# Conv transposes and dt steps placed behind chosen projection products, and dt results stored by direction, in a Fourier and SSD mixer layer

## The chip, the cores and the metric

One core of a Trainium2 chip runs the whole layer in one launch. The metric is the device time in microseconds. TensorE is called PE, VectorE DVE, ScalarE ACT, GpSimd POOL and SyncE SP; all transfers here are issued by SP, in its program order.

## What is computed

One layer over 2048 latent and 256 context tokens of width 1024. The normed and modulated input is multiplied by one input projection, whose columns are split five ways; two mixers read them, and one output projection adds the result to the input.

```python
u, zf, zs, xbc, dt_raw = jnp.split(h @ w_in, PROJ_SPLITS, axis=-1)
four = fourier_mixer(u, zf, w_fourier, b_fourier)
xbc = depthwise_conv_grid(xbc, conv_w, conv_b, rows, cols)
ssd, h_f, h_b = ssd_mixer(xbc, dt_raw, zs, dt_bias, a_log, d_skip, ssd_norm_w, h0_f, h0_b)
```

`dt` is softplus(dt_raw + bias) for 24 heads and two directions. The SSD scan works on chunks of 128 tokens: 16 of the latent sequence and 2 of the context. It needs, for each chunk, the cumulative sum of dt x A, its total, and exponentials of them. The convolution is a depthwise 3 x 3 over a 32 x 64 grid (over one row of 256 for the context), with a SiLU.

## The kernel before

A product of two float32 operands is made of three TensorE products of high and low parts (hh x wh, hl x wh, hh x wl), so a projection of one channel tile (128 channels) over 512 tokens is 24 products of 128x512 (L170 to L172). The program is written with a tile framework: buffers come from pools with a fixed count, and a scheduler decides, within the dependencies, in which order each engine's instructions stand. An engine's order is then fixed, and an instruction that waits holds up all that stand behind it on that engine. `tc.issue_after(x)` adds edges: what is created under it stands behind instruction x.

The stages that the change touches, with their times in the profile:

- The u stage, about 116 to 275 us. A loop over n2 in 0..15 (L465) projects 128 tokens on 512 channels with 24 u-products (L474 to L476), splits the result, and multiplies it by a DFT matrix with three products (L482 to L484) into a "tr" accumulator, which DVE copies to "gs" (L486) for a store. The context block (`ctx_block`, called at n2 = 2) transposes the normed context (L236), splits it on DVE, ACT and POOL (L238, L72, L68), and makes its dt_raw (L252, L253). `dt_part(i)` is called at n2 = 4, 7 and 10, each for six of the 18 chunks. It loads transposed dt_raw from DRAM into "ev" buffers, of which there are two (L412), adds bias and softplus on DVE and ACT after products with an identity (L414), makes cumulative sums and totals on PE (L433, L436), stores four results to `sm_d` (L447), and transposes the cumulative sum and the log of dt less that sum by groups of up to four chunks (L455); ACT and DVE write the high and low halves of each group to "ev" (L457, L458), which are stored to `cum_d` and `q_d`.
- The conv stage, about 270 to 835 us. `conv_tile` is called for 20 channel tiles in CONV_ORDER (a C, a B and three x tiles, four times). A tile has four blocks of 512 tokens; ACT copies each block to an image (`img`), of which there are two. `finish(half)`, called after block 2 and block 3, lets ACT make the first tap (L561), DVE the other eight (L564), and ACT the SiLU (L567), on one of two "acc" buffers (four "cacc" and "acc" in all, by kind). It returns a function that transposes the eight token tiles (L509), copies them (L511) and stores them; B tiles also multiply with the C tile's result (L539) and reduce its diagonal on POOL and DVE (L544, L545) to `cbd`. These functions wait in a list, `late`, and one is called after each odd block. x and B tiles end with the context: 24 products, two taps, SiLU (L604), two transposes.
- The start of the scan, about 820 to 905 us. `zf_tile(2)` projects one more tile; then `sml`, `ecb` and `dtb2` are loaded from `sm_d`, DVE makes `dsc` from `dtb2` and `cbd` (L631), and the scan steps begin, with projections of zs tiles between them and gate steps (L757 to L764) that load a weight each.

PSUM has five "mm" accumulators for projections (`main_psum`), two "tr" ones (`tr_psum`) and one for the context. The later stages are the rest of the scan (to about 1160 us), the Fourier mixer (to about 1300) and the output stage; of the change they see only where the dt results are loaded from, and a slightly different order.

Of the kernel before, what the change touches and what calls it, by code (L numbers as in the profile page):

```python
# [18 lines left out]
P = 128  # L19
# [7 lines left out]
H = 24  # L27
# [22 lines left out]
def mixer_layer(ctx: ExitStack, tc: tile.TileContext, A: dict, out: bass.AP, taps=None):  # L50
# [36 lines left out]
    sm_d = scratch("sm_d", [NALL, P, 4, W2])  # L87
# [68 lines left out]

    def weights(idx, raw=None):
# [9 lines left out]
    def project_k(po, w, hi, lo, c0, n, k):  # L167
        wh, wl = w
        a, b = hi[:, k, c0:c0 + n], lo[:, k, c0:c0 + n]
        mm(po, wh[:, k], a, start=(k == 0), stop=False)  # L170
        mm(po, wh[:, k], b, start=False, stop=False)  # L171
        mm(po, wl[:, k], a, start=False, stop=(k == KT - 1))  # L172
# [177 lines left out]
    with ExitStack() as pu:  # L350
# [48 lines left out]
        def dt_part(i):  # L399
            sl = slice(NH * i, NH * i + NH)  # L400
# [3 lines left out]

            def bc(t):
                return t.unsqueeze(1).broadcast_to([P, NH, W2])

            pt = tr_psum([P, NH, W2])
            for q0 in range(0, NH, 4):
# [3 lines left out]
                for q in range(nq):  # L413
                    mm(pt[:, q0 + q, :], dtT[:, q * P:(q + 1) * P], D0["i2"], start=True, stop=True)  # L414
            v, e, u, s1_, dtt, wdec, etot, ecum = (D0[t].rearrange("p (c w) -> p c w", w=W2) for t in
                                                   ("v", "e", "u", "s1", "dtt", "wdec", "etot", "ecum"))
            nc.vector.tensor_tensor(out=v, in0=pt, in1=bc(D0["dtb"]), op=ALU.add)
# [11 lines left out]
            da, cum = u, e  # L429
            nc.vector.tensor_tensor(out=da, in0=dtt, in1=bc(D0["nega"]), op=ALU.mult)  # L430
            pt = tr_psum([P, NH, W2])
            for d, tri in enumerate(("triu", "tril")):
                mm(pt[:, :, d * H:(d + 1) * H], D0[tri], da[:, :, d * H:(d + 1) * H], start=True, stop=True)  # L433
            nc.vector.tensor_copy(out=cum, in_=pt)
            pt = tr_psum([P, NH, W2])
            mm(pt, D0["ones"], da, start=True, stop=True)  # L436
            nc.scalar.activation(etot, pt, AF.Exp)
            nc.vector.tensor_tensor(out=wdec, in0=pt, in1=cum, op=ALU.subtract)
            nc.scalar.activation(wdec, wdec, AF.Exp)
            nc.vector.tensor_tensor(out=wdec, in0=wdec, in1=dtt, op=ALU.mult)  # L440
            nc.scalar.activation(ecum, cum, AF.Exp)
            lq = v
            nc.vector.tensor_scalar(out=lq, in0=dtt, scalar1=1e-37, scalar2=None, op0=ALU.max)
            nc.scalar.activation(lq, lq, AF.Ln)
            nc.vector.tensor_tensor(out=lq, in0=lq, in1=cum, op=ALU.subtract)
            for q, t in enumerate((wdec, etot, ecum, dtt)):
                store(sm_d[sl, :, q].rearrange("c p w -> p c w"), t)  # L447
            for src, dst in ((cum, cum_d), (lq, q_d)):
                c0 = NH * i
                while c0 < min(NH * (i + 1), NCH):  # L450
                    nq = min(4, min(NH * (i + 1), NCH) - c0)
                    n = nq * P
                    pt = tr_psum([W2, 512])
                    for q in range(nq):
                        nc.tensor.transpose(pt[:, q * P:(q + 1) * P], src[:, c0 + q - NH * i], ident)  # L455
# [7 lines left out]

        dt_consts()
        for n2 in range(16):  # L465
            if n2 == 2:
                ctx_block()
            if n2 in (4, 7, 10):
                dt_part((n2 - 4) // 3)
            po = main_psum()  # L470
            for k in range(KT):
# [4 lines left out]
                mm(po, b, wuh[:, k], start=False, stop=(k == KT - 1))  # L476
# [14 lines left out]
    with ExitStack() as pc_:  # L491
# [57 lines left out]
        def conv_tile(n, ci):  # L549
# [34 lines left out]
            for b in range(4):  # L584
# [20 lines left out]
            (x_tokens if kind == "x" else b_tokens)(acc, j, NCH, NCC)  # L605

        late = []
# [12 lines left out]
    sml = pers.tile([P, NALL, 2, W2], F32, name="sml")  # L620
    ecb = pers.tile([P, NCH, H], F32, name="ecb")
    dsc = pers.tile([P, NCH, G, HG], F32, name="dsc")

    zf_tile(2)
    dtb2 = pers.tile([P, NCH, H], F32, name="dtb2")
    dsk = const_tile("dskip", pers)
    smr = sm_d[:].rearrange("c p i w -> p c i w")
    load(sml, smr[:, :, 0:2])
    load(ecb, smr[:, :NCH, 2, H:])
    load(dtb2, smr[:, :NCH, 3, H:])  # L630
    nc.vector.tensor_tensor(out=dsc, in0=dtb2[:].rearrange("p c (g h) -> p c g h", g=G),  # L631
# [695 lines left out]
```

## Time and profile before

| | |
|---|---|
| median of three runs | 1951.25 us (1950.36 to 1951.3) |
| profiled execution | 1953.2 us, of which the span is 1951.2 us |
| mean granted PE clock | 0.979 |
| DVE, ACT, POOL busy | 70%, 44%, 47% of the span |
| DMA | 269.77 MB in 279,826 packets, 138 GB/s |

In lines of the profile a group is named by the source line, the engine, the operation and output <- inputs. In a line of waits, "PE ptr L482 <- DVE ev L458" says that PE's instruction of line 482 stood still until DVE's of line 458 was done. The time of a wait is idle time of the waiting engine only.

### The profile page before, as it was taken

The numbers are of one execution on the slowest core, as the hardware profiler recorded it, in microseconds if no ns is written. First come the engines' busy times: TensorE is split into PE (matmuls) and PEld (weight loads), VectorE is DVE, ScalarE is ACT, GpSimd is POOL, SyncE is SP. The second block draws the span as 40 slices with busy tenths as digits, with TensorE's granted clock in tenths as the row PEclk, the third lists the DMA queues.
The fourth block names the chain that finished last, engine by engine and source line by source line (L and its number), as shares of the span: only waits on it lengthen the run. The fifth ranks groups of instructions, "written<-read, shape, count | busy, mean of one in ns | idle before, by whom it ended". The sixth has DMA issues, their size and how long they took to land.

```text
span 1951.2 us, 27816 instructions
## 1 busy us (share of the span) xinstructions
PE 1826.5 (94%) x9142; PEld 1498.0 (77%) x9142; DVE 1374.8 (70%) x1830; ACT 863.6 (44%) x1940; POOL 919.3 (47%) x766
## 2 busy tenths in 40 slices
PE   6999799999999998998999999988899999999997
PEld 2798687787887887877788886865678777777776
DVE  3743357999898998947666641357878887778874
ACT  3631124443444444425566654335544444444442
POOL 1321023314114023137777762256877776777742
PEclk9999799999999999998999999999999999999998
DMA  7332322323223233276777766476544444444441
GB/s 275 138 102 57 77 77 78 104 76 106 73 68 102 71 90 106 63 210 188 224 221 237 215 196 218 146 226 202 163 131 147 137 140 131 138 143 134 139 141 40
DMA packets 279826, 269.77 MB, mean 138 GB/s; under 512 B 38818, under 2 KB 247586, under 8 KB 279171
## 3 DMA queue, kind: packets, MB, share of 16 engines
q1 hardware_dynamic: 279682, 268.00, 45.7%
q8 instruction: 73, 1.20, 0.3%
q14 instruction: 71, 0.57, 0.1%
HBM read 181.37 MB, written 86.54 MB: 137 GB/s over the span
## 4 chain that ended last, share of the span: by engine, by line
PE 33%; DVE 24%; POOL 8%; DMA 7%; issue 6%; ACT 4%; SPq 1%; POOLq 0%; ACTq 0%; DVEq 0%
DVE acc L564 17%; PE po L1167 5%; PE po L1165 5%; PE po L1166 5%; PE pj L171 3%; PE pj L172 3%; PE pj L170 3%; PE py L1106 2%; DMA wo<-in_wout 2%; DMA xt<-xtok_d 2%; POOL yb L730 1%; PE parg L1032 1%; POOL xw L710 1%; SPq L63 1%; POOL wl L72 1%
## 5 line engine op out<-in xcount | busy, mean ns | idle before, releaser
L564 DVE SCALAR_TENSOR_TENSOR acc<-img,c_convw,acc 128x1024 f32<-128x1024 f32 x320 | 478.8, 1511 | 32.9 <-ACT acc L561 24.3
L172 PE MATMUL pj<-hh,wl 128*128 128x512 f32 x1152 | 456.6, 396 | 0.9 <-POOL wl L72 0.9
L171 PE MATMUL pj<-hl,wh 128*128 128x512 f32 x1152 | 455.5, 395 | 0.0
L170 PE MATMUL pj<-hh,wh 128*128 128x512 f32 x1152 | 452.3, 396 | 0.0
L72 POOL TENSOR_TENSOR wl<-raw,wh 128x1024 fp32r<-128x1024 f32 x48 | 123.7, 2578 | 443.1 <-ACT wh L68 443.1
L172 PEld LDWEIGHTS pj<-hh,wl 128*128 128x128 f32 x1152 | 218.2, 189 | 47.5 <-POOL wl L72 1.5
L170 PEld LDWEIGHTS pj<-hh,wh 128*128 128x128 f32 x1152 | 218.9, 190 | 41.1 <-issue 1.2
L171 PEld LDWEIGHTS pj<-hl,wh 128*128 128x128 f32 x1152 | 218.5, 190 | 41.3 <-issue 1.6
L1165 PE MATMUL po<-hl,mh 128*128 128x512 f32 x384 | 155.6, 405 | 4.6 <-ACT mh L68 2.1
L1166 PE MATMUL po<-hh,mh 128*128 128x512 f32 x384 | 152.5, 397 | 2.2 <-DVE hh L810 2.2
L1167 PE MATMUL po<-hl,ml 128*128 128x512 f32 x384 | 146.0, 398 | 1.5 <-POOL ml L72 1.5
L727 ACT ACTIVATE xd<-xt,dsc 128x64 f32<-128x64 f32 x384 | 101.1, 336 | 82.8 <-POOL yb L730 80.7
L1032 PE MATMUL parg<-rt,lt 128*128 128x384 f32 x256 | 90.0, 374 | 14.8 <-DVE parg L1034 10.5
L1036 ACT ACTIVATE w<-parg 128x384 f32<-128x384 f32 x128 | 62.3, 487 | 89.8 <-DVE parg L1034 89.4
L567 ACT ACTIVATE acc<-acc,c_convb 128x1024 f32<-128x1024 f32 x40 | 46.1, 1152 | 116.8 <-DVE acc L564 116.8
L72 POOL TENSOR_TENSOR ml<-gt,mh 128x384 fp32r<-128x384 f32 x64 | 68.8, 1075 | 60.6 <-ACT mh L68 58.2
L710 POOL TENSOR_TENSOR xw<-xt,sml 128x384 f32<-128x384 f32 x76 | 67.0, 883 | 53.8 <-DVE xl L72 38.9
L1037 DVE TENSOR_TENSOR w<-w,cb 128x768 f32<-128x768 f32 x64 | 83.3, 1301 | 12.2 <-ACT w L1036 11.4
L68 ACT ACTIVATE xh<-xw 128x384 fp32r<-128x384 f32 x136 | 70.0, 515 | 47.9 <-POOL xw L710 18.4
L1075 POOL TENSOR_TENSOR ts<-ts,yb 128x384 f32<-128x384 f32 x64 | 71.4, 1116 | 40.9 <-issue 16.3
L1034 DVE COPY_PREDICATED parg<-msk,parg 128x384 f32<-128x384 uint8 x128 | 70.8, 553 | 26.5 <-PE parg L1032 26.3
L72 POOL TENSOR_TENSOR sl<-hf,sh 128x384 fp32r<-128x384 f32 x64 | 77.4, 1210 | 22.8 <-ACT sh L68 19.9
(375 smaller groups left out, 4044.2 us busy)
## 6 DMA issues: line engine op xcount, KB each, us to landing
raw<-in_win SPq DMA_DIRECT2D x48, 512.0 KB
xt<-xtok_d SPq DMA_DIRECT2D x80, 192.0 KB
xtok_d<-tk SPq DMA_DIRECT2D x48, 256.0 KB
zsT_d<-ev SPq DMA_DIRECT2D x48, 256.0 KB
yb_d<-yb SPq DMA_DIRECT2D x64, 192.0 KB
yb<-yb_d SPq DMA_DIRECT2D x64, 192.0 KB
zs<-zsT_d SPq DMA_DIRECT2D x64, 192.0 KB
xg<-xtok_d SPq DMA_DIRECT2D x64, 192.0 KB
```

The lines of the kernel that those rows point to most:

```text
L72: (lo_engine or nc.vector).tensor_tensor(out=lo, in0=src, in1=hi.bitcast(F32), op=ALU.subtract)
L170: mm(po, wh[:, k], a, start=(k == 0), stop=False)
L171: mm(po, wh[:, k], b, start=False, stop=False)
L172: mm(po, wl[:, k], a, start=False, stop=(k == KT - 1))
L564: nc.vector.scalar_tensor_tensor(out=acc, in0=im[:, r0 + dy:r0 + dy + 16, dx:dx + GRID_W], scalar=tap(t), in1=acc, op0=ALU.mult, op1=ALU.add)
L710: nc.gpsimd.tensor_tensor(out=xw, in0=xt, in1=wd, op=ALU.mult)
L727: nc.scalar.activation(xd[:, h], d["x"][:, h], AF.Copy, scale=dsc[:, c, g, h:h + 1])
L1032: mm(po, l[:, dr], r[:, cols], start=True, stop=True)
L1037: nc.vector.tensor_tensor(out=w, in0=w, in1=cb[:].unsqueeze(1).broadcast_to([P, HG, P]), op=ALU.mult)
L1165: mm(po, a, wh[:, i], start=(g == 0 and q == 0), stop=False)
L1166: mm(po, a, wl[:, i], start=False, stop=False)
L1167: mm(po, b, wh[:, i], start=False, stop=(g == 3 and q == 3))
```

## The change

Three things are done.

First, `dt_part` is cut into three steps: `dt_soft` (load, identity products, softplus), `dt_cum` (sums, exponentials, stores) and `dt_rows` (transposes, splits, stores). For part i they are called at n2 = 3 + 4i, 5 + 4i and 6 + 4i, each behind an edge from the last u-product of that n2. Their accumulators come from the five "mm" buffers instead of the two "tr" ones.

Second, in the conv stage the transposing functions go into two lists by block. `flush` calls them behind an edge from the last projection product before it: after block 1 those of the first half, after block 3 those of the second half and of the context, each of the tile before. The last z_f tile is moved into the conv section, so that the last conv tile's functions stand behind its blocks 1 and 3.

Third, `sm_d` becomes `smf_d` and `smb_d`, one for each direction, with the partition first. A dt part writes seven stores instead of four; the scan loads `smb` (one run of 6912 bytes for each partition) and the two context chunks of `smf` instead of `sml`, `ecb` and `dtb2`, and `dsc` is made in place in a part of `smb`. The output stage loads 288 bytes for each partition and chunk instead of 768.

The core of the diff:

```diff
-            pt = tr_psum([P, NH, W2])
+            pt = dt_psum()
...
             for q, t in enumerate((wdec, etot, ecum, dtt)):
-                store(sm_d[sl, :, q].rearrange("c p w -> p c w"), t)
-            for src, dst in ((cum, cum_d), (lq, q_d)):
+                if q < 3:
+                    store(smf_d[:, sl, q], dview(t)[:, 0])
+                store(smb_d[:, q, sl], dview(t)[:, 1])
+
+        def dt_rows(i):
+            for src, dst in ((D0["e"], cum_d), (D0["s1"], q_d)):
...
+                    pt = main_psum()[:W2]
...
+        dt_work = {3 + 4 * i + q: (fn, i) for i in range(3) for q, fn in ((0, dt_soft), (2, dt_cum), (3, dt_rows))}
         for n2 in range(16):
             if n2 == 2:
                 ctx_block()
-            if n2 in (4, 7, 10):
-                dt_part((n2 - 4) // 3)
...
+                mu = mm(po, b, wuh[:, k], start=False, stop=(k == KT - 1)).ins
+            if n2 in dt_work:
+                fn, i = dt_work[n2]
+                with tc.issue_after(mu):
+                    fn(i)
...
-                if b % 2 and late:
-                    late.pop(0)()
+                if b % 2:
+                    flush(b)
                 if b == 2:
-                    late.append(finish(0))
+                    late[1].append(finish(0))
                 if b == 3:
-                    late.append(finish(1))
+                    late[3].append(finish(1))
...
-            (x_tokens if kind == "x" else b_tokens)(acc, j, NCH, NCC)
+            late[3].append(lambda: (x_tokens if kind == "x" else b_tokens)(acc, j, NCH, NCC))
...
+        def flush(b):
+            with tc.issue_after(done["mm"]):
+                while late[b]:
+                    late[b].pop(0)()
+
         for n, ci in enumerate(CONV_ORDER):
             conv_tile(n, ci)
-        for fn in late:
-            fn()
+        w = weights(6)
+        for b in range(4):
+            plain_block(w, b, AF.Silu, zf_sink(2))
+            if b % 2:
+                flush(b)
...
-    load(sml, smr[:, :, 0:2])
-    load(ecb, smr[:, :NCH, 2, H:])
-    load(dtb2, smr[:, :NCH, 3, H:])
+    load(smf, smf_d[:, NCH:, 0:2])
+    load(smb, smb_d)
```

How the order moves. In the u stage, around part 0 of before (line 433 makes the cumulative sums, 455 the row transposes, 482 to 484 the DFT products), PE's rows are:

```order
L433 MATMUL ptr<-wh,wl 128x6x24 x2
L436 MATMUL ptr<-wh,wl 128x288
L455 MATMUL ptr<-c_ident,wh 48x128 x12
L482 MATMUL ptr<-uh,h_dft_1088 128x512
L483 MATMUL ptr<-ul,h_dft_1088 128x512
L484 MATMUL ptr<-uh,l_dft_1089 128x512
```

and around the row transposes of the second part after (line 472; 490 to 492 are u-products, 502 to 504 the DFT):

```order
L491 MATMUL pj<-wul,hh 128x512
L492 MATMUL pj<-wuh,hl 128x512
L472 MATMUL pj<-c_ident,wh 48x128 x6
L472 MATMUL pj<-c_ident,wl 48x128 x6
L502 MATMUL ptr<-uh,h_dft_1089 128x512
L503 MATMUL ptr<-ul,h_dft_1089 128x512
L504 MATMUL ptr<-uh,l_dft_1090 128x512
L490 MATMUL pj<-wuh,hh 128x512
```

The sums (now line 446) have left the row transposes by 24 products, and u-products of the next n2 follow one DFT triple behind the transposes.

The context block stood among u-products in before (236 transposes, 252 and 253 dt products):

```order
L474 MATMUL pj<-wuh,hh 128x512
L236 MATMUL ptr<-c_ident,rawu 128x128
L236 MATMUL ptr<-c_ident,rawv 128x128
L475 MATMUL pj<-wul,hh 128x512
L252 MATMUL pc<-hch,wdt 96x256
L476 MATMUL pj<-wuh,hl 128x512
L474 MATMUL pj<-wuh,hh 128x512
L236 MATMUL ptr<-c_ident,rawu 128x128
L236 MATMUL ptr<-c_ident,rawv 128x128
L253 MATMUL pc<-hcl,wdt 96x256
```

Now its transposes (239) and dt products (255, 256) follow each other with no u-product between them; the first softplus product stands behind them:

```order
L239 MATMUL ptr<-c_ident,rawu 128x128
L239 MATMUL ptr<-c_ident,rawv 128x128
L239 MATMUL ptr<-c_ident,rawu 128x128
L239 MATMUL ptr<-c_ident,rawv 128x128
L255 MATMUL pc<-hch,wdt 96x256
L239 MATMUL ptr<-c_ident,rawu 128x128
L239 MATMUL ptr<-c_ident,rawv 128x128
L256 MATMUL pc<-hcl,wdt 96x256
L255 MATMUL pc<-hch,wdt 96x256
L239 MATMUL ptr<-c_ident,rawu 128x128
```

In the conv stage, at the boundary of two x tiles, ACT's rows in before (561 is the first tap, 567 the SiLU of a half; "tk" copies are those of transposed tokens, "img" those of projected blocks):

```order
L68 ACTIVATE img_2030<-pj 128x8x64
L68 ACTIVATE tk<-ptr 128x512 x2
L561 ACTIVATE acc<-img_2030,c_convw 128x1024
L68 ACTIVATE img_2030<-pj 128x8x64
L68 ACTIVATE tk<-ptr 128x256
L68 ACTIVATE img_2030<-pj 128x8x64
L567 ACTIVATE acc<-acc,c_convb 128x1024
```

and after, at such a boundary (581 is the first tap, 587 the SiLU):

```order
L68 ACTIVATE img_2040<-pj 128x8x64
L68 ACTIVATE tk<-ptr 128x512 x2
L581 ACTIVATE acc<-img_2040,c_convw 128x1024
L587 ACTIVATE acc<-acc,c_convb 128x1024
L68 ACTIVATE img_2040<-pj 128x8x64 x2
L68 ACTIVATE tk<-ptr 128x512 x2
L581 ACTIVATE acc<-img_2040,c_convw 128x1024
```

The two token copies of a half stand behind the image copy of block 1 and then behind that of block 3, and the first tap of a half follows them at once. On PE this is a set of eight transposes after every 48 projections; in before the sets of the repeating part stood 34 to 38 projections after the one before within a tile, and some 47 after it from tile to tile, among the context products.

At the end of the stage the last tile's two halves now stand between the blocks of the last z_f tile and the last context transposes 24 products later, and the first scan steps stand with 47 projections among them (64 before), after which nine follow without a projection between (seven before).

More of the change, by code (lines that the diff above doesn't have):

```diff
@@ L155, in ctx_psum @@
         return ps.tile([P, CTX], F32, name="pc", tag="cx", bufs=1)
+    done = {}
     def weights(idx, raw=None):
@@ L171, in project_k @@
         mm(po, wh[:, k], b, start=False, stop=False)
-        mm(po, wl[:, k], a, start=False, stop=(k == KT - 1))
+        done["mm"] = mm(po, wl[:, k], a, start=False, stop=(k == KT - 1)).ins
     def project(po, w, hi, lo, c0, n):
@@ L413, in dt_part @@
                 for q in range(nq):
[L414 to L417, printed above, removed]
+                    mm(dview(pt)[:, :, q0 + q], dtT[:, q * P:(q + 1) * P], D0["i2"], start=True, stop=True)
+            v, e, u, s1_, dtt = (D0[t] for t in ("v", "e", "u", "s1", "dtt"))
+            nc.vector.tensor_tensor(out=dview(v), in0=dview(pt), in1=dbc("dtb"), op=ALU.add)
             nc.vector.scalar_tensor_tensor(out=e, in0=v, scalar=-1.0, in1=v, op0=ALU.mult, op1=ALU.max)
@@ L428, in dt_part, with dt_cum @@
             nc.vector.scalar_tensor_tensor(out=dtt, in0=v, scalar=0.0, in1=s1_, op0=ALU.max, op1=ALU.add)
-            da, cum = u, e
-            nc.vector.tensor_tensor(out=da, in0=dtt, in1=bc(D0["nega"]), op=ALU.mult)
-            pt = tr_psum([P, NH, W2])
+            nc.vector.tensor_tensor(out=dview(u), in0=dview(dtt), in1=dbc("nega"), op=ALU.mult)
+        def dt_cum(i):
+            da, cum, lq = (D0[t] for t in ("u", "e", "v"))
+            dtt, wdec, etot, ecum = (D0[t] for t in ("dtt", "wdec", "etot", "ecum"))
+            pt = dt_psum()
@@ L619, in mixer_layer, with scan_sm @@
     pers = pool("pers", stack=pp_)
[L620 to L625, printed above, removed]
-    dsk = const_tile("dskip", pers)
-    smr = sm_d[:].rearrange("c p i w -> p c i w")
-    load(sml, smr[:, :, 0:2])
-    load(ecb, smr[:, :NCH, 2, H:])
-    load(dtb2, smr[:, :NCH, 3, H:])
-    nc.vector.tensor_tensor(out=dsc, in0=dtb2[:].rearrange("p c (g h) -> p c g h", g=G),
-                            in1=cbd[:].unsqueeze(3).broadcast_to([P, NCH, G, HG]), op=ALU.mult)
-    dv = dsc[:].rearrange("p c g h -> p c (g h)")
+    smb = pers.tile([P, 4, NALL, H], F32, name="smb")
+    smf = pers.tile([P, NCC, 2, H], F32, name="smf")
+    dsk = const_tile("dskip", pers)
+    load(smf, smf_d[:, NCH:, 0:2])
+    load(smb, smb_d)
+    dv = smb[:, 3, :NCH]
+    dv4 = dv.rearrange("p c (g h) -> p c g h", g=G)
+    nc.vector.tensor_tensor(out=dv4, in0=dv4, in1=cbd[:].unsqueeze(3).broadcast_to([P, NCH, G, HG]), op=ALU.mult)
     nc.vector.tensor_tensor(out=dv, in0=dv, in1=dsk[:].unsqueeze(1).broadcast_to([P, NCH, H]), op=ALU.add)
+    def scan_sm(dr, q, c, g):
+        t = smb[:, q, c] if dr else smf[:, c - NCH, q]
+        return t[:, g * HG:(g + 1) * HG].unsqueeze(2).broadcast_to([P, HG, 64])
     zw = {}
@@ L1007, in s1 @@
         if g == 0:
-            sml = wa1.tile([P, 4, W2], F32, name="sml4", tag="sml")
-            load(sml, sm_d[c])
+            sml = wa1.tile([P, 3, H], F32, name="sml4", tag="sml")
+            load(sml, smf_d[:, c])
         else:
```

52 lines of the change are left out of this document (27 added, 25 removed).

## The prediction

> **What bounds the kernel now.** I read the page's engine table first, then windows stage by stage, then the waits of TensorE (PE), and last the timelines of the stalls. On the page the columns are busy time, share of the span and instructions.
>
> ```profile
> PE 1826.5 (94%) x9142; PEld 1498.0 (77%) x9142; DVE 1374.8 (70%) x1830; ACT 863.6 (44%) x1940; POOL 919.3 (47%) x766
> ```
>
> PE is busy for 94% of the span, so nearly everywhere PE's own work sets the end, and what can be won is the time in which it stands still or runs at a lower clock. The windows of the stages that the change touches say how much that is. Columns: window, its length, busy time of PE, weight loads, DVE, ACT and POOL with instruction counts, then granted clock, DMA share and GB/s.
>
> ```profile
> 190.00:210.00 20.00, 12.90 (x51) 9.80 (x48) 6.94 (x13) 4.36 (x10) 0.00 (x0) 0.74 0.44 107
> 224.00:244.00 20.00, 13.20 (x51) 9.91 (x51) 7.36 (x14) 4.75 (x10) 0.00 (x0) 0.74 0.43 106
> 258.00:270.00 12.00, 10.64 (x49) 8.12 (x49) 6.78 (x13) 5.66 (x11) 6.72 (x5) 1.00 0.64 157
> ...
> 320.00:340.00 20.00, 16.53 (x87) 14.27 (x87) 10.66 (x9) 7.60 (x13) 5.50 (x4) 0.83 0.23 63
> 340.00:450.00 110.00, 106.99 (x540) 89.21 (x540) 105.44 (x79) 48.98 (x74) 27.82 (x15) 1.00 0.32 91
> 450.00:470.00 20.00, 15.97 (x77) 13.14 (x76) 19.72 (x14) 6.94 (x12) 5.69 (x4) 0.91 0.31 88
> 470.00:560.00 90.00, 88.24 (x462) 74.67 (x461) 78.17 (x61) 42.21 (x64) 21.02 (x11) 1.00 0.30 82
> 560.00:700.00 140.00, 134.60 (x689) 113.60 (x688) 127.20 (x94) 60.62 (x90) 35.29 (x18) 1.00 0.31 87
> 700.00:840.00 140.00, 134.87 (x684) 113.74 (x683) 123.53 (x90) 59.45 (x89) 34.14 (x18) 0.99 0.32 89
> ...
> 860.00:905.00 45.00, 35.94 (x140) 28.11 (x139) 28.39 (x42) 18.68 (x49) 28.93 (x30) 0.85 0.63 188
> ```
>
> Idle time is length less PE's busy time; clock loss is length times (1 − clock). The first three windows are the three dt parts of the u stage: idle 7.10 + 6.80 + 1.36 = 15.3 us, clock 0.26 x 20 twice = 10.4 us, so 25.7 us. The next six are the conv stage: idle 3.47 + 3.01 + 4.03 + 1.76 + 5.40 + 5.13 = 22.8 us, clock 3.4 + 1.8 + 1.4 = 6.6 us, so 29.4 us. The last is the start of the scan: 9.1 us idle and 0.15 x 45 = 6.8 us of clock, 15.8 us. Together 71 us are within reach of the change. The waits of PE name what it stood for in the u stage (us in total, times, longest):
>
> ```profile
> PE ptr L482 <- DVE ev L458: 6.9, 5, 2.4
> PE ptr L455 <- DVE ev L458: 6.8, 4, 2.8
> ```
>
> and in the conv stage:
>
> ```profile
> PE ptr L509 <- ACT acc L567: 18.2, 11, 4.0
> PE ptr L509 <- ACT accc L604: 4.1, 3, 1.4
> ```
>
> **The u stage, what goes.** In before the row transposes (L455) and the DFT products behind them (L482) share the two "tr" accumulators, and these come free only as the two "ev" buffers do. PE's timeline of part 0 (start, duration, instruction, idle time before):
>
> ```profile
> 187.97 0.40 PE L475 MATMUL pj<-wul,hh 128*128 128x512 f32 x1
> 188.20 0.40 PE L476 MATMUL pj<-wuh,hl 128*128 128x512 f32 x1
> ...
> 195.05 0.40 PE L455 MATMUL ptr<-c_ident,wh 128*48 128x128 f32 x2 [2.77 <-DVE ev L458]
> 197.86 0.79 PE L482 MATMUL ptr<-uh,h_dft 128*128 128x512 f32 x1 [2.41 <-DVE ev L458]
> ```
>
> and ACT's, which shows why: each copy out of an accumulator waits until a store has emptied a buffer.
>
> ```profile
> 190.31 0.58 ACT L68 ACTIVATE ev<-ptr 48x512 fp32r<-48x512 f32 x1
> ...
> 194.04 0.38 ACT L68 ACTIVATE ev<-ptr 48x256 fp32r<-48x256 f32 x1 [2.82 <-DMA cum_d<-ev]
> 196.50 0.59 ACT L68 ACTIVATE ev<-ptr 48x512 fp32r<-48x512 f32 x1 [2.08 <-DMA cum_d<-ev]
> 199.14 0.38 ACT L68 ACTIVATE ev<-ptr 48x256 fp32r<-48x256 f32 x1 [2.05 <-DMA q_d<-ev]
> ```
>
> The change moves these accumulators to the five "mm" ones and puts the DFT elsewhere, so the four row groups no longer hold up PE: I take all 25.7 us as gone.
>
> **The u stage, what comes.** The ring of two "ev" buffers is as slow as before: 199.14 − 190.31 = 8.8 us for four groups. SyncE's queue then issues the next part's load:
>
> ```profile
> 201.25 0.30 SPq L63 DMA_DIRECT2D ev<-dtT_d  x1
> ```
>
> That is 10.9 us after the first copy, and a load needs about 2 us more (an estimate from the 2.05 to 2.82 us that ACT waited for stores): 13 us. In after, the first softplus product (L424) of the next part stands behind only twelve transposes, 24 u-products and two DFT triples: 30 x 0.23 us (188.20 − 187.97) + 12 x 0.11 = 8.3 to 8.6 us. So PE waits about 4.4 us, twice (parts 1 and 2): 8.8 us. Behind L424 all further u-products are queued, so nothing covers it. The first L424 has no row ring before it, but its load is queued on SyncE behind a store of "gs"; I take 2.5 us, between nothing and the 2.82 us of the ACT row. The context block comes in one piece (see the section on the change). Its pace is that of three engines on two buffers (busy, mean ns):
>
> ```profile
> L238 DVE TENSOR_SCALAR gs<-ptr,scl,mod 128x256 f32<-128x256 f32 x8 | 4.4, 544 | 15.0 <-PE ptr L236 15.0
> L72 POOL TENSOR_TENSOR hcl<-gs,hch 128x256 fp32r<-128x256 f32 x5 | 3.7, 737 | 30.6 <-ACT hch L68 30.6
> L68 ACT ACTIVATE hch<-gs 128x256 fp32r<-128x256 f32 x8 | 3.4, 419 | 19.4 <-DVE gs L238 19.4
> ```
>
> Eight steps of 0.54 + 0.42 us are 7.7 us, against 16 transposes and 16 short dt products of about 0.11 us each, 3.6 us: 4 us of waiting that before hid among u-products. The three cumulative sums (L446) stand a full block behind their softplus; I cost them at nothing, at most 2 us each. Sum of new waits: 8.8 + 2.5 + 4 = 15.3 us.
>
> The clock comes on top. In the conv stage a gap of 3.47 us (first row below) was followed by products 0.43 us apart (the next two), against 0.23:
>
> ```profile
> 326.85 1.97 PE L509 MATMUL ptr<-c_ident,acc 128*128 128x128 f32 x8 [3.47 <-ACT acc L567]
> ...
> 329.04 0.63 PE L171 MATMUL pj<-hl,wh 128*128 128x512 f32 x1
> 329.47 0.63 PE L172 MATMUL pj<-hh,wl 128*128 128x512 f32 x1
> ```
>
> while the 5.40 us of shorter gaps in 560:700 left it at 1.00. That stall of 3.47 us lost 3.4 us of clock in its window, that of 4.03 us 1.8. The two new waits of 4.4 us I charge with 2.4 us together, between 0 (as in 560:700) and 6.8 (twice 3.4). So 17.7 us of the 25.7 come back: the u stage gains **8 us**, with ends at −2 (sums wait 2 us each, 4 us more of clock) and 22 (only the context block waits). [...]
>
> **The conv stage.** All waits here are transposes (L509) that stand in PE's queue before ACT's Silu (L567) is done; the projections behind them need nothing. In after each set stands behind the last projection of block 1 or block 3. In the repeating part it moves from 34 to 48 projections behind the previous set, 14 x 0.23 = 3.2 us later, more than most gaps there. What could be late next is DVE, whose taps feed the Silu: in 560:700 it works 127.2 us, and PE needs 134.6 without its idle time, so DVE would be 94.5% busy and PE still last. Its own waits there and in the rest of the stage:
>
> ```profile
> DVE acc L564 <- ACT acc L561: 24.3, 9, 3.5
> DVE cbd L545 <- POOL dg L544: 23.3, 7, 9.8
> ```
>
> 47.6 us in 560 us, or 11.9 in 140. The first is for ACT, which waits for PE's image, and shrinks with PE's period; of the second some stays. I leave 3.4 us of stalls, at the B tiles, where products and tokens meet: gain **26 us**; ends 13 (below, second case) and 29.4. The context transposes move too, behind a block of the next tile, with more room than before.
>
> **Start of the scan.** The loads of dt results become two. In before their many small packets left DVE standing at the queue's head:
>
> ```profile
> DVE dsc L631 <- DMA dtb<-sm_d: 15.2, 1, 15.2
> ```
>
> and PE then waited:
>
> ```profile
> PE ptr L764 <- DVE gate L761: 2.8, 1, 2.8
> PE ptr L740 <- DVE hf L750: 2.3, 1, 2.3
> ```
>
> The earlier dt data help the 2.3 us. Against it, the last context tokens now come some 24 projections into the last z_f tile, the first "xt" loads are queued behind their stores, and nine scan steps instead of seven follow each other without projections between. I call it **0**, between +8 (about half of 15.8) and −6 (two more steps at the 2.3 to 2.8 us of the waits above). After the scan PE is again the bound. The order of the output stage changes a little between its first and last third; I cost it at nothing, 4 us either way. The seven stores per dt part instead of four run beside u-products at a DMA share of 0.44: nothing on the path.
>
> Sum: 8 + 26 + 0 = 34 us. From the profiled execution's 1953.2 us that is 1919.2; the median of the runs is 1.95 us below that execution, so the forecast is **1917 us**.
>
> **The rivals.** First, the forecast, 0.55, between 1905 and 1928 by the ends above.
>
> Second, DVE becomes the bound of the conv stage. For: 94.5%, and its wait for POOL. Against: most of its waits hang on PE. If 10 of its 12.8 idle us per 140 us stay, the period is 127.2 + 10 = 137.2 and the gain 2.8 instead of 5.4, half: 13 us in all, total 21, **1930 us**, 0.17.
>
> Third, the start of the scan shrinks as well. For: DVE's 15.2 us wait, and the DMA was nearly full. If 11 of 15.8 us go, the total is 45: **1906 us**, 0.14. [...]
>
> Fourth, slower: the two accumulators "acc" are held longer. Each set of transposes moved 3.2 us later frees its buffer later, and ACT's first tap (L561), with DVE behind it, must wait. Against: the buffer freed behind block 3 is wanted only after it, when DVE still has the other half. Per five tiles (ten halves) DVE has 12.8 us to spare before the conv stage is slower than now, 1.3 us a half; at 1.9 us a half the loss is 6.2 us for five tiles, 25 for twenty, less 8 us from the u stage: 17 us, **1968 us**, 0.09.
>
> Fifth, the waits only change places: the u stage comes out even and each conv transpose still stands as long behind its Silu. **1950 us**, 0.05.
>
> **Numbers.** 0.2%, some 4 us, is about what a measurement of this kernel can tell from no change. Faster by more: first to third, 0.86. Within it: 0.05. Slower: 0.09. The range 1900 to 1941 holds the first three with their ends and leaves out 0.14 and the far ends.
>
> **What would show it.** Right: in 280 to 820 us hardly any wait of PE for ACT's acc and DVE at 93 to 96%; in the u stage waits for "ev" loads in front of L424, a few us each; the scan's start as long as now. Wrong: DVE over 97% in the conv stage with PE waiting (second); ACT's L561 waiting for transposes (fourth); waits in the u stage over 20 us; a scan start that loses less than 8 us (third).

## The result and the profile after

The changed kernel takes 1962.36 us (median of 5 runs, 1958.24 to 1965.7), the kernel before beside it 1950.36 us (1946.32 to 1951.3): a ratio of 1.0066, 95% interval 1.0047 to 1.0086. It is slower by 12 us where 34 us less were forecast. The profiled execution takes 1965.7 us with a span of 1963.9 us. The page has PE busy for longer, at the same share of the span:

```profile
PE 1843.1 (94%) x9142; PEld 1507.1 (77%) x9142; DVE 1387.7 (71%) x1830; ACT 856.7 (44%) x1940; POOL 918.2 (47%) x766
```

Both kernels have the same 9142 products on PE, so a product's number is a clock of progress. The table has the start of product n (counted from 0) in the changed kernel less that in the kernel before, from the two traces, and the change of that difference in the stage that ends there.

| product | end of | start before, us | after less before, us | stage, us |
|---|---|---|---|---|
| 400 | prologue | 100.0 | +1.4 | +1.4 |
| 1200 | u stage, start of conv stage | 298.1 | +8.6 | +7.2 |
| 3600 | nearly all of the conv stage | 793.3 | +2.4 | -6.2 |
| 5200 | scan | 1154.6 | +0.3 | -2.1 |
| 9141 | Fourier and output stage | 1942.1 | +12.3 | +12.0 |

The 1.4 us of the prologue are not the change's: every kernel profiled below, with that part unchanged, has 1 to 3 us there (two with other accumulators more).

**u stage.** Windows of the stage, first of before and then of after (columns as in the prediction):

```profile
140.00:290.00 150.00, 134.67 (x587) 118.38 (x586) 64.26 (x106) 32.03 (x61) 16.01 (x12) 0.93 0.28 72
```

```profile
140.00:290.00 150.00, 133.68 (x555) 116.52 (x554) 64.44 (x108) 28.73 (x58) 12.78 (x11) 0.91 0.25 67
```

PE is idle for 16.3 us where it was for 15.3, and its granted clock, 0.91 where it was 0.93, costs 0.09 x 150 = 13.5 us where it cost 10.5. In the same 150 us it gets 32 fewer products done. PE's waits there after:

```profile
PE pj L424 <- DMA ev<-dtT_d: 7.3, 3, 3.1
PE ptr L502 <- ACT uh L68: 3.9, 5, 1.6
PE ptr L239 <- DVE gs L241: 1.9, 1, 1.9
PE ptr L503 <- DVE ul L500: 1.6, 3, 0.6
PE pj L446 <- DVE wh L438: 1.1, 1, 1.1
```

The row transposes no longer wait, but what stands behind them does. ACT's timeline shows the ring of ev buffers at the same pace as before, now with the copy of the next u block queued behind it:

```profile
188.73 0.38 ACT L68 ACTIVATE ev<-pj 48x256 fp32r<-48x256 f32 x1 [2.34 <-DMA cum_d<-ev]
191.20 0.59 ACT L68 ACTIVATE ev<-pj 48x512 fp32r<-48x512 f32 x1 [2.09 <-DMA cum_d<-ev]
193.85 0.38 ACT L68 ACTIVATE ev<-pj 48x256 fp32r<-48x256 f32 x1 [2.06 <-DMA q_d<-ev]
194.13 0.58 ACT L68 ACTIVATE uh<-pj 128x512 fp32r<-128x512 f32 x1
```

and PE's has the DFT product that needs that block, then the softplus product that needs the load behind the ring:

```profile
194.76 0.50 PE L502 MATMUL ptr<-uh,h_dft 128*128 128x512 f32 x1 [1.64 <-ACT uh L68]
...
198.54 1.91 PE L424 MATMUL pj<-wh,ev 96*128 96x48 f32 x8 [2.08 <-DMA ev<-dtT_d]
```

**Conv stage.** PE's idle time falls only from 22.8 to 17.0 us. Its window and its waits after:

```profile
280.00:840.00 560.00, 542.98 (x2739) 458.34 (x2738) 507.31 (x369) 231.69 (x356) 144.75 (x72) 0.99 0.29 83
```

```profile
PE ptr L529 <- ACT acc L587: 10.3, 5, 3.2
PE ptr L529 <- ACT tk L68: 6.1, 3, 2.5
```

More than half of the waits for the SiLU are still there (18.2 us before), and a new kind has come, for the copies of transposed tokens ("tk") out of the two "tr" accumulators. ACT itself now stands far longer in front of the SiLU, waiting for DVE's taps; the first line is of before, the second of after:

```profile
ACT acc L567 <- DVE acc L564: 116.8, 38, 7.2
ACT acc L587 <- DVE acc L584: 217.2, 39, 8.2
```

The gain is all at the beginning of the stage: 10.5 us up to product 2000, after which, up to product 3600, the changed kernel takes 4.3 us more than the kernel before.

**Output stage.** Most of the loss is in the one stage where the change only loads less. It falls between products 6400 and 7200 (+0.4 to +10.8 us), at some 1426 to 1584 us. One stall stands out; the first fence is PE's timeline after, the second POOL's, the third SyncE's queue:

```profile
1478.36 0.39 PE L1190 MATMUL po<-hh,mh 128*128 128x512 f32 x1
1481.97 1.22 PE L1191 MATMUL po<-hl,ml 128*128 128x512 f32 x2 [3.22 <-POOL ml L72]
```

```profile
1480.14 0.83 POOL L1110 TENSOR_TENSOR xw<-xg,sml 128x384 f32<-128x384 f32 x1 [4.58 <-DMA xg<-xtok_d]
1480.92 0.99 POOL L72 TENSOR_TENSOR ml<-gt,mh 128x384 fp32r<-128x384 f32 x1
```

```profile
1475.47 0.33 SPq L63 DMA_DIRECT2D xr<-in_x  x1
1475.89 0.38 SPq L63 DMA_DIRECT2D xg<-xtok_d  x1
```

PE waits for POOL's low half "ml", which stands on POOL behind a multiply that waits for "xg", whose load SyncE issued only after those of the residual rows "xr". In the kernel before (first line, 1400 to 1750 us) the waits for "ml" are short, after (second line, 1400 to 1700 us) one of 3.2 us stands out:

```profile
PE po L1167 <- POOL ml L72: 1.5, 2, 1.0
PE po L1191 <- POOL ml L72: 3.9, 2, 3.2
```

From 1481 to 1487 us, about the end of this stall, the granted clock is 0.50. A window around it of before, then of after:

```profile
1480.00:1500.00 20.00, 20.00 (x115) 16.83 (x114) 16.20 (x26) 9.73 (x25) 16.71 (x17) 1.00 0.43 126
```

```profile
1480.00:1500.00 20.00, 18.03 (x89) 14.55 (x90) 8.82 (x15) 6.31 (x17) 10.46 (x11) 0.83 0.24 71
```

26 products fewer in 20 us are some 4.5 us of work, at the 115 products in 20 us of before.

### The profile page after: what moved, and what is told of

It is laid out like the page before. It is cut to its first block, busy times and chain, and to the rows that moved or that the text cites. A ratio compares the mean times of both kernels' runs of the same rounds, so it can differ in the third digit from the quotient of the medians.

```text
span 1963.9 us, 27837 instructions
## 1 busy us (share of the span) xinstructions
PE 1843.1 (94%) x9142; PEld 1507.1 (77%) x9142; DVE 1387.7 (71%) x1830; ACT 856.7 (44%) x1940; POOL 918.2 (47%) x766
## 4 chain that ended last, share of the span: by engine, by line
PE 63%; DVE 19%; DMA 7%; issue 4%; ACT 3%; POOL 3%; SPq 1%; DVEq 0%; ACTq 0%; POOLq 0%
DVE acc L584 12%; PE pj L174 9%; PE pj L175 9%; PE pj L173 9%; PE po L1191 5%; PE po L1189 5%; PE po L1190 5%; PE py L1130 2%; PE pj L490 2%; PE parg L1056 1%; PE pj L492 1%; PE pj L491 1%; DMA xg<-xtok_d 1%; PE py L1133 1%; PE ptr L529 1%
## 5 line engine op out<-in xcount | busy, mean ns | idle before, releaser
L584 DVE SCALAR_TENSOR_TENSOR acc<-img,c_convw,acc 128x1024 f32<-128x1024 f32 x320 | 483.8, 1519 | 40.3 <-ACT acc L581 30.4
L752 ACT ACTIVATE xd<-xt,smb 128x64 f32<-128x64 f32 x384 | 101.1, 336 | 76.1 <-POOL yb L756 63.3
L1061 DVE TENSOR_TENSOR w<-w,cb 128x768 f32<-128x768 f32 x64 | 82.5, 1289 | 14.4 <-ACT w L1060 11.3
L72 DVE TENSOR_TENSOR xl<-xw,xh 128x384 fp32r<-128x384 f32 x76 | 65.9, 868 | 32.3 <-ACT xh L68 32.0
L1189 PEld LDWEIGHTS po<-hl,mh 128*128 128x128 f32 x384 | 73.7, 192 | 19.4 <-ACT mh L68 4.1
```

What stands on the lines that cost most here:

```text
L72: (lo_engine or nc.vector).tensor_tensor(out=lo, in0=src, in1=hi.bitcast(F32), op=ALU.subtract)
L584: nc.vector.scalar_tensor_tensor(out=acc, in0=im[:, r0 + dy:r0 + dy + 16, dx:dx + GRID_W], scalar=tap(t), in1=acc, op0=ALU.mult, op1=ALU.add)
L752: nc.scalar.activation(xd[:, h], d["x"][:, h], AF.Copy, scale=smb[:, 3, c, g * HG + h:g * HG + h + 1])
L1061: nc.vector.tensor_tensor(out=w, in0=w, in1=cb[:].unsqueeze(1).broadcast_to([P, HG, P]), op=ALU.mult)
L1189: mm(po, a, wh[:, i], start=(g == 0 and q == 0), stop=False)
```

## The experiments

For each run the table has its ratio to the kernel before, measured beside it, with the 95% interval, and the change in each stage by the count of products as above, in us against the kernel before.

| run | ratio | u | conv | scan | Fourier, output |
|---|---|---|---|---|---|
| the changed kernel | 1.0066 (1.0047 to 1.0086) | +7.2 | -6.2 | -2.1 | +12.0 |
| e1 before, one more load | 1.0050 (1.0032 to 1.0068) | -0.9 | -0.7 | -2.4 | +6.4 |
| e2 conv part alone | 1.0028 (1.0013 to 1.0043) | +0.5 | -1.9 | +0.3 | +4.2 |
| e3 layout alone | 1.0009 (0.9991 to 1.0026) | +1.5 | -1.6 | -6.6 | +0.8 |
| e4 after, fewer taps | 1.0011 (0.9997 to 1.0026) | +4.7 | -16.3 | +2.0 | +7.3 |
| e5 after without conv part | 1.0020 (1.0007 to 1.0033) | +7.3 | -6.0 | -10.6 | +6.7 |
| e6 after, halves in one | 1.0002 (0.9992 to 1.0012) | -1.9 | -6.4 | +0.2 | +4.1 |
| e7 before, halves in one | 0.9976 (0.9964 to 0.9989) | -8.1 | -1.0 | -4.6 | +3.6 |
| e8 after, C x B x x | 1.0064 (1.0044 to 1.0085) | +7.8 | -8.2 | +0.3 | +8.2 |
| e9 e6 with z_f tile back | 1.0018 (1.0007 to 1.0029) | -2.2 | -6.7 | -1.9 | +6.3 |
| e10 e6 with tr 3, mm 4 | 0.9970 (0.9956 to 0.9983) | -7.6 | -9.8 | -4.0 | +9.5 |
| e11 before, layout and halves | 0.9978 (0.9964 to 0.9992) | -4.6 | -1.4 | -8.6 | +1.3 |
| e12 e11 with tr 3, mm 4 | 0.9933 (0.9916 to 0.9949) | -17.2 | +1.9 | -7.6 | +3.7 |
| e13 after, four xr buffers | 1.0020 (1.0007 to 1.0033) | +4.0 | -6.2 | -1.9 | +1.1 |
| e14 before, twelve more stores | 1.0037 (1.0024 to 1.0051) | +2.3 | +0.1 | -2.2 | +2.7 |

The stages come from one profiled execution each, and a profiled execution can lie several us from the median of its kernel (that of e3 is 4.3 us below it, that of the changed kernel 3.3 above). Stages in which PE's products stand in the order of the kernel before differ from it by up to 3 us, and the scan of e7 by 4.6: the scans of e1, e7 and e14, all with that order, come out 2.2 to 4.6 us shorter than the one profile of before. A smaller difference in one stage shows nothing by itself.

**e1: the output stage's order alone.** The prologue loads the identity twice.

```diff
+            load(ident, A["ident"])
             load(ident, A["ident"])
```

> The kernel before with one thing more: the 64 KB identity is loaded a second time in the prologue. No product, layout or edge is changed, but the scheduler's order of the output stage comes out nearly as in the changed kernel (between products 5500 and 7000 of 8480), while u and conv stage keep their order. Theory P (plan): the 11 us that the changed kernel loses between about 1480 and 1540 us come from the new order of the output stage alone. It expects 1955 to 1963 us here, with the loss at about 1460 to 1560 us. Rival L (layout): they come from the loads out of the new DRAM layout; it expects 1950 us, no change, and no loss in the output stage.

1959.29 us against 1948.78. Behind the prologue no stage up to product 5200 is longer than in the kernel before; from there to product 7600 it loses 8.6 us. The wait is the one seen after the change:

```profile
PE po L1168 <- POOL ml L72: 4.2, 3, 2.8
```

So a load that changes no result costs 10 us by the medians; 6.4 us of it show in the Fourier and output stage of its profile, through the order that the scheduler gives to a stage 1300 us later. Theory P holds: the changed layout is not needed for that loss.

**e2: the conv part alone**, on the kernel before: `flush` with its edges, the lists, and the z_f tile moved, as in the diff above.

> The kernel before with the conv part alone: the two lists, the edges behind blocks 1 and 3, the context tokens behind block 3, the last z_f tile moved into the conv section. dt parts and DRAM layout are as before. Theory P with D (the conv stage is bound by DVE while C, B and the first x tile pass, so that transposes moved behind more projections wait for the same Silu): some 6 us gained between 280 and 350 us, nothing or 1 to 2 us a group lost after that, and 5 to 12 us lost in the output stage: 1952 to 1962 us. My prediction's own view, that the edges take away the waits, would give some 26 us less in the conv stage: about 1925 us. Rival L: no loss in the output stage, since the layout is the old one: about 1946 us.

1955.13 us. The conv stage gains 1.9 us, not 26, and not the 6 us that theory P allowed for its beginning either; the output stage loses 4.2. The waits hardly fall (18.2 us for the SiLU before), and those for token copies are new:

```profile
PE ptr L511 <- ACT acc L569: 15.6, 7, 3.8
PE ptr L511 <- ACT tk L68: 3.8, 2, 2.0
```

Layout and dt parts are old here, so the loss in the output stage speaks against rival L again.

**e3: the layout alone**, with `smf_d` and `smb_d` and their loads.

> The kernel before with the DRAM layout by direction alone: seven stores for each dt part, smb and smf loaded for the scan, 288 bytes for each partition and chunk in the output stage. Steps, edges and conv stage as before. Theory P: u and conv stages as before, the start of the scan within 3 us, output stage 5 to 12 us longer through its new order: 1953 to 1963 us. Rival L expects the same loss, so this run tells only with the others; if the start of the scan gains 8 us or more, the third case of the prediction was right on that point.

1952.79 us, not to be told from no change in the total. The start of the scan and the scan gain 6.6 us together, of which 2.2 to 4.6 are also seen with an unchanged scan (see above). DVE's wait for dt results, 15.2 us before, is halved:

```profile
DVE smb L631 <- DMA smb<-smb_d: 7.5, 1, 7.5
```

The output stage lost 0.8 us, less than theory P expected, though between products 6400 and 7600 its order is that of e1.

**e4: fewer taps.** This leaves out three of nine taps for the C channels.

```diff
-                for t in (0, 1, 2, 3, 5, 6, 7, 8):
+                for t in ((0, 1, 2, 3, 5) if kind == "C" else (0, 1, 2, 3, 5, 6, 7, 8)):
```

> The changed kernel with five DVE taps instead of eight on the four C tiles, so part of the convolution of the C channels is left out; PE's order is the same. DVE works 3 x 1.5 us less on each half, 9 us less for a group of five tiles, while PE's work stays. Theory D (DVE sets the pace from the C tile to the first x tile): PE's waits for the Silu after the B tile go, and the group's period of 140.2 us falls to 134 to 137 us, 12 to 20 us less for the stage, 1942 to 1950 us. Rival E (the edges themselves hold PE, whatever DVE does): under 4 us, 1958 us or more.

1951.69 us, 11 less than the changed kernel; the conv stage is 10.1 us shorter. That is less than the 12 to 20 expected and well above what rival E allowed. Over some two and a half groups between products 2000 and 3600 the time is 320.7 us (324.1 before, 328.4 after), so leaving out 24 taps, which takes 41.5 us from DVE's busy time (1387.7 to 1346.2 us), saves 10. What is left has changed its kind:

```profile
PE ptr L529 <- ACT tk L68: 10.0, 5, 2.6
PE ptr L529 <- ACT acc L587: 2.5, 3, 0.9
```

The waits for the SiLU go with DVE's work, and waits for token copies take their place.

**e5: the changed kernel without its conv part.**

> The changed kernel with its conv part undone: dt steps behind u-products and the layout by direction stay, the conv stage and the z_f tile are as in the kernel before. If the u stage lost its 7 us by the split dt steps (waits for loads of dtT, and the clock), the same loss stands here between 140 and 300 us, and with the layout's gain at the start of the scan (4 us) and the new order of the output stage (6 to 10 us lost) the run takes 1953 to 1962 us. If the loss in the u stage had come from something of the conv part (weights loaded earlier, say), the u stage would be as in the kernel before and the run 1946 to 1953 us.

1954.01 us. The u stage loses its 7 us here too. With the layout alone (e3) it lost 1.5, so the split of the dt parts is the cause. And the conv stage, in the old form, gains the same 6.0 us, 6.5 of them up to product 2000: what looked like the gain of the edges comes with the split dt parts, at the first conv tiles. PE comes to its first set of conv transposes at the same time as before (323.55 us against 323.38), 42 products earlier in its order, and the SiLU is done 2.4 us sooner: of the stall of 3.47 us at 326.85, 0.89 us are left.

```profile
324.44 1.09 PE L529 MATMUL ptr<-c_ident,acc 128*128 128x128 f32 x8 [0.89 <-ACT acc L587]
```

By e2, and by the changed kernel against this run, the edges are worth 0 to 2 us in the conv stage.

**e6 and e7: high and low half in one ev buffer**, on the changed kernel and on the kernel before.

```diff
-                    th, tl = (evac_tile()[:W2].bitcast(F32R) for _ in range(2))
+                    rw = evac_tile()
+                    th, tl = (rw[r:r + W2].bitcast(F32R) for r in (0, 64))
```

> The changed kernel with the high and the low half of a row group in one ev buffer, on partitions 0 to 47 and 64 to 111, so that two groups fit into the ring instead of one. Theory R (the ring of ev buffers, behind which the next dtT load stands, makes PE wait at the softplus products of parts 1 and 2 and drops the clock there): those two waits of 2.1 us go, and at least one stretch at half clock of 6.8 us with each: 6 to 10 us less in the u stage, 1953 to 1957 us. Rival Q (the load is late by its place in SyncE's queue and by its own latency, not by the ring): under 2 us, 1960 us or more.

> The kernel before with the high and the low half of a row group in one ev buffer, nothing else. The stalls of the dt parts (idle 13.9 and clock 10.4 us in parts 0 and 1) are those of the ring by my reading: two groups of four then pass without a wait, and 10 to 18 us go from the u stage. The order of the output stage changes to that of the changed kernel (9 us lost there): 1940 to 1949 us. If the stalls are rather those of stores that SyncE issues one after another, under 5 us go, and with the output stage's loss the run takes 1954 us or more.

e6 takes 1951.11 us, 11 less than the changed kernel, and its u stage is 9.1 us shorter. Theory R holds in the sum, but not by the wait that it named. The loads still wait:

```profile
PE pj L424 <- DMA ev<-dtT_d: 6.4, 3, 3.2
```

What went are most of the waits for ACT's copy of the u block (3.9 to 1.6 us) and a third of the clock loss (0.91 to 0.94 in 140 to 290 us). In all, PE's idle time in the stage falls by 4.0 us, and what half clock costs while PE works by 4.4. e7 takes 1945.91 us and its u stage gains 8.1 us, a little under the range expected: it has one long wait of 3 us in each part in place of three. It is the first kernel here that is faster than the one before, by 0.24%.

**e8: another order of the tiles.**

```diff
-CONV_ORDER = [16, 12, 0, 1, 2, 17, 13, 3, 4, 5, 18, 14, 6, 7, 8, 19, 15, 9, 10, 11]
+CONV_ORDER = [16, 0, 12, 1, 2, 17, 3, 13, 4, 5, 18, 6, 14, 7, 8, 19, 9, 15, 10, 11]
```

> The changed kernel with the conv tiles in another order: in each group an x tile stands between C and B (C x B x x instead of C B x x x); the order of u and output stage is the same. Theory D (DVE falls behind where C, B and the first x tile follow each other, since a C tile gives PE 96 products against 120 and DVE the same sixteen taps, and cannot work ahead in the x tiles): the shortfall of C is made up before B comes, PE's waits shrink by 1 to 4 us a group: 1948 to 1958 us. Rival A (what counts is the work of DVE in a group, wherever it stands, or the edges): within 3 us of the changed kernel, 1959 to 1965 us.

1963.16 us, no change against the changed kernel. Theory D fails in this form: an x tile between C and B does not help. DVE now stands for the diagonal of the B tile's products instead (first line: the changed kernel):

```profile
DVE cbd L565 <- POOL dg L564: 17.4, 4, 4.4
DVE cbd L565 <- POOL dg L564: 39.5, 4, 10.6
```

**e9 and e10, both on e6: the z_f tile put back (e9), and three accumulators for transposes (e10, whose edit follows).**

```diff
-        return ps.tile([P, 512], F32, name="pj", tag="mm", bufs=5)
+        return ps.tile([P, 512], F32, name="pj", tag="mm", bufs=4)
...
-        return ps.tile(shape, F32, name="ptr", tag="tr", bufs=2)
+        return ps.tile(shape, F32, name="ptr", tag="tr", bufs=3)
```

> The changed kernel with the halves of a row group in one ev buffer, and with the last z_f tile put back behind the conv section, so that the last conv tile's transposes stand before it and not among its blocks. Theory Z (the layout alone gains 4 to 8 us at the start of the scan, as in the runs without the conv part, and the moved tile gives them back, because the last tokens and so the first loads of xt come later): from product 3600 to 4400 this run gains 4 to 8 us where the same kernel with the tile moved gained nothing; with the output stage's order unknown, 1942 to 1948 us. Rival: the start of the scan stays as long, 1951 us.

> The changed kernel with the halves of a row group in one ev buffer, and with three accumulators for transposes and four for products instead of two and five. Theory S (in the conv stage the transposes wait for token copies on ACT, which stand behind a SiLU that waits for DVE, and all sets now stand where this meets them): with one more accumulator the waits of PE for token copies go and half of the rest, 3 to 8 us less between products 1200 and 3600. Rival D (DVE's work sets the pace, whatever accumulators there are): under 2 us there, or longer, since a block's image copy must free its accumulator sooner. The u stage may lose some us by the missing accumulator, so the stage and not the total decides.

e9 takes 1952.5 us. From product 3600 to 4400 it gains 1.4 us where e6 lost 2.3, so 3.7 us, just under the range; over the whole scan 2.1. The layout without the conv part gains 6.6 to 10.6 us there (e3, e5), so the moved tile explains at most part of what is missing, and 2.1 us are no more than what unchanged scans differ by.

e10 takes 1945.52 us. Between products 1200 and 3600 it is 3.3 us shorter than e6, at the low end of theory S, and the waits for token copies are gone (5.4 us in e6):

```profile
PE ptr L530 <- ACT acc L588: 13.8, 7, 3.0
PE ptr L530 <- ACT tk L68: 0.8, 2, 0.4
```

The waits for the SiLU rise from 10.5 to 13.8 us: more than half of what the copies gave up. The u stage, where a loss was feared, gained 5.7 us against e6; the prologue lost 4.

**e11 and e12: what helps, without the edges.**

> The kernel before with two things: the DRAM layout by direction and the halves of a row group in one ev buffer. dt parts, conv stage and z_f tile stay where they were. If the gains seen apart add up, 8 us in the u stage and 4 to 7 us around the start of the scan, less 4 to 9 us for another order of the output stage: 1938 to 1946 us, faster than both kernels. If the scan's gain was chance, 1946 us.

> The kernel before with the DRAM layout by direction, the halves of a row group in one ev buffer, and three accumulators for transposes and four for products. If the third transpose accumulator also helps where the sets of transposes stand freely, as in the kernel before, the conv stage loses 3 to 8 us of waits and the run takes 1937 to 1943 us. If it helps only where the edges put sets of transposes behind a waiting SiLU, the conv stage stays and the four product accumulators cost a little in the prologue: 1945 to 1950 us.

e11 takes 1945.26 us, no better in the total than e7. e12 takes 1937.71 us, 0.9933 of the kernel before (0.9916 to 0.9949), the fastest kernel of this study. The conv stage did not gain, as its second alternative said, but the u stage did, which neither expected: its window is nearly full at full clock.

```profile
140.00:290.00 150.00, 145.78 (x662) 129.59 (x661) 85.24 (x122) 39.23 (x70) 19.89 (x15) 1.00 0.32 79
```

It has 662 products in 150 us against 587. As I read it, the third accumulator lets the DFT products pass while two are held by row groups, but the order of the u stage moved with it, and no run separates the two. That is what the change wanted from the "mm" accumulators, without moving a dt step.

**e13 and e14: the output stage again.** e13 gives "xr" four buffers (and its tag's other use as well); e14 is the kernel before with each dt result stored in two halves.

```diff
-            ost["xr"] = [wk.tile([P, 512], F32, name="xr", tag="xr") for _ in range(2)]
+            ost["xr"] = [wk.tile([P, 512], F32, name="xr", tag="xr", bufs=4) for _ in range(2)]
```

> The changed kernel with four buffers instead of two for the residual rows xr of the output stage. Theory X (the output stage loses its 11 us because a load of xg stands in SyncE's queue behind loads of xr, which wait until the stores of the two xr buffers are done, and POOL, then PE, wait for xg): with free buffers these loads no longer wait, the waits of PE for POOL's ml go, and the output stage from product 6400 on is 5 to 12 us shorter, 1950 to 1957 us. Rival: the order that the scheduler makes is what costs, wherever its waits are; the order changes again, and the stage comes out within 4 us: 1958 us or more.

> The kernel before with each of the four dt results stored in two stores, one for each direction, into the same layout: twelve more stores in the u stage. Nothing else is changed, but the order of the output stage comes out far from both (some 2000 of its products at other places). If any order other than that of the kernel before costs, as the one extra load showed for one such order, the output stage is 4 to 12 us longer and the run takes 1954 to 1962 us; if orders differ by chance in both directions, it lies within 4 us or is shorter. The u stage should be within 2 us of the kernel before.

e13 takes 1955.47 us; from product 6400 on it loses 3.2 us against the kernel before, the changed kernel 11.9, and the wait for "ml" is

```profile
PE po L1191 <- POOL ml L72: 1.5, 3, 0.8
```

against 3.9 in the same stretch (1400 to 1700 us). That is as theory X expected, but the order changed with the buffers, so it does not show the queue behind "xr" to be the reason, let alone the only one. e14 takes 1956.87 us, with 2.7 us in the output stage of its profile and 2.3 in the u stage, between the two expectations.

These runs hold fewer orders than it seems. Between products 6400 and 7600 the changed kernel and e1 to e12 have PE's products in one order, and the other engines' instructions too but for a few of SyncE's transfers; the kernel before, e13 and e14 have three others. In all thirteen profiles with the one order PE stands for "ml" at the same product, 6681, for 1.2 to 4.0 us; in the other three no wait for "ml" in that stretch is longer than 1.3 us. So the stall belongs to the order, not to the change. What it costs scatters: against the kernel before, the thirteen lose 2.5 to 11.2 us between these products, the changed kernel most of all. There PE is idle for 12.7 us where it was for 7.6, and half clock costs 4.6 us where it cost nothing; in e3, with the same order, it is 9.0 us and nothing. e13 and e14 lost 5.5 and 0.9 us. No order here did better than that of the kernel before, but four orders are few.

## Why the prediction was wrong

**The u stage** (forecast 8 us less, measured 7.2 more). The step that failed is the clock's term: "The two new waits of 4.4 us I charge with 2.4 us together, between 0 ... and 6.8". The idle time came out as forecast, 16.3 us against 15.3, if by other waits: the softplus products waited 7.3 us and not 11.3, the context block 1.9 and not 4, and the copy of the next u block, which stands on ACT behind the ring, 3.9 us that were not in the sum. But the clock was at half for as long as costs 13.5 us. The trace has it at 0.50 in 157 to 163, 198 to 204 and 235.5 to 241.5 us, about the softplus products' waits of 3.1, 2.1 and 2.1 us, and in two shorter stretches besides: 27 us in all, where the two stalls of the kernel before had 20. And the reckoning "idle plus clock" counts twice: while PE is idle, half clock costs nothing more. Taking half of PE's busy time in the stretches at half clock, the loss between products 400 and 1200 is 7.2 us before (of 10.2 by the clock alone) and 12.9 after (of 13.7). So the 25.7 us "within reach" were some 3 us too many, and 5.7 us of clock and 1.0 of idle time make 6.7 of the 7.2. (The sum of 8.3 to 8.6 us in front of L424 comes to 8.2, which changes little.) e5 shows the loss with the dt steps alone, e6 that the ring behind it is the main cause.

**The conv stage** (26 us less, measured 6.2, of which the edges made 0 to 2). The step that failed is "DVE would be 94.5% busy and PE still last". It took an average over five tiles for each moment's bound. DVE is busy for only 90.6% of 280 to 840 us after, and PE still waits 10.3 us for the SiLU; by e4, where less work of DVE takes most of these waits away, they are the moments at which DVE is behind. Moving the transposes 3.2 us later in PE's queue did not outlast them, and what was held behind the SiLU on ACT, the token copies, is now waited for as well (6.1 us). e4 shows DVE's share (10 us for 24 taps), e10 the accumulators' (3 us). That DVE is behind only where C and B follow each other was my theory afterwards, and e8 speaks against it. Two rivals came near. The second had DVE behind, but its sign, DVE over 97% busy, did not come. The fifth, that the waits only change places, had 1950 us and a chance of 0.05; it fits the conv stage, where PE waited 22.3 us for SiLUs before and 16.4 us for SiLUs and token copies after. What would free the rest of the stage was not found.

**The start of the scan** (0, measured -2.1 over the scan): right in size, as far as one profile can tell. The third rival counted on 11 us from the layout. DVE's wait did halve (e3), and the profiles without the conv part have 6.6 to 10.6 us (e3, e5, e11), of which unchanged scans have 2.2 to 4.6 as well. The totals do not settle it: e3 is 8 us below e1, whose order it shares between products 6400 and 7600, but e11 is no faster than e7. With the conv part little of it is left (-2.1); e9 puts about 2 us of that on the moved z_f tile, within the noise, and the rest stays open.

**The output stage** ("I cost it at nothing, 4 us either way", measured +12.0 with the Fourier stage). This is the term that turned the sign. The step that failed is the price of nothing for a new order: a stall of 3.2 us that the kernel before does not have, other longer waits and the clock, 0.83 in 1480 to 1500 us where it was 1.00. Without this term the profile would show no difference that a measurement can tell: 1.4 + 7.2 - 6.2 - 2.1 = 0.3 us. e1 shows that such an order comes without any of the change, and costs: 10 us by the medians, 6.4 in its profile. That it is 12.0 in this profile is in part this execution, 3.3 us above its median; the twelve other profiles with that order have 0.8 to 9.5 us behind product 5200. None of the rivals named it; the fourth, held "acc" buffers, and its 1968 us had nothing to do with the loss.

## What to carry to other kernels

Where a scheduler makes the order, any edit, even one more load, can reorder a stage far from it; compare the orders of all stages, and measure an edit that changes only the order before a difference is put down to what was meant. A wait that is moved behind more work of its own engine goes only if what it waits for is not itself the slower stream there, and the queue of the engine between (here ACT) decides what waits next: 10.3 of the 18.2 us of waits for the SiLU stayed, and 6.1 us for token copies came. Ask first for one more buffer at the place where the ring is full: a third accumulator and two halves in one buffer, with the layout, gave 0.67%, where the moved steps cost 0.66%.

## What the runs showed of the hardware

In the changed kernel no wait of PE in the u stage is longer than 3.1 us, and the granted clock of 140 to 290 us is 0.91, lower than before (0.93, longest wait 2.8 us). In e12, where the longest is 0.9 us, it is 1.00:

```profile
PE ptr L486 <- DVE gs L490: 1.8, 2, 0.9
```

The length of a wait alone does not tell the clock. In the changed kernel a wait of 1.9 us that ends at 145.3 us stands beside a granted clock of 0.50 in 146.5 to 149.5 us, while with one of 3.15 us that ends at 462.3 us it is 1.00 over 455 to 495 us. Three waits of 1.6, 0.5 and 2.1 us, the last ending at 198.5 us, stand beside 0.50 in 198 to 204 us; in the kernel before one of 3.47 us, ending at 326.9 us, stands beside 0.50 in 326 to 332 us. So a few short waits close together went with half clock here, as one longer wait did.
